# Mixer of an encoder block: wider token projections, decay products by direction, LayerNorm factors behind the transposes

## The chip, the cores and the metric

The kernel runs on one core of a Trainium2 chip. The metric is the device time of one launch in microseconds (us). Engines are named as the profile names them: PE is TensorE (PEld its weight loads), DVE is VectorE, ACT is ScalarE, POOL is GpSimd, SP is the engine whose queue issues most DMAs.

## The reference, cut to what matters

256 tokens (S) of 1024 channels (D), all float32. The block has two parts: a mixer with three branches, and 32 experts of which each token takes four.

```python
h = layer_norm(x, ln_in_g, ln_in_b)
mem_n = layer_norm(mem, ln_mem_g, ln_mem_b)
proj = h @ w_in + b_in          # q, k, v, r, lr_f, lr_b, fn, mq, gates
la_f = log_sigmoid(lr_f @ w_decay_f + b_decay_f) / 16    # lr_f: [256, 16]
la_b = log_sigmoid(lr_b @ w_decay_b + b_decay_b) / 16
# A) gated linear attention over q, k, v, la_f forward and over the flipped ones with la_b
# B) 2-D DFT of fn      C) cross-attention of mq into mem_n @ w_mem_kv
merged = g0 * y_gla + g1 * y_fnet + g2 * y_mem
h = layer_norm(alpha * h + merged @ w_out + b_out, ln1_g, ln1_b)
h = layer_norm(alpha * h + moe(h), ln2_g, ln2_b)
```

where `layer_norm(x) = (x - mean) * rsqrt(var + eps) * g + b`, by rows of 1024.

## The kernel before

The function `block` calls `mixer` and then `moe`. The experts' weights (2 MB a load) go into ten ring buffers; six of them are freed during the mixer and loaded early (`early_load`, line 777).

**Projections.** Every projection is done in split precision: ScalarE copies a weight chunk of 128x1024 into a rounded format (`whi`, line 117), VectorE subtracts to get the rest (`wlo`, line 118), and each product is three matmuls (`mm3`, lines 144 to 146): high by high, high by low, low by high. The activations h are kept split and transposed as `hT`, the memory as `mT`. There are four buffers of `whi` and of `wlo`, and three of raw weights.

`project_T` gives a result with channels on the partitions: the weight chunk is stationary, 256 tokens move. `project_tok` (line 325) gives a result with tokens on the partitions: 128 tokens of the activations are stationary, the weights move. It is called five times: twice for v, once for the memory's values, twice for the output projection. A call covers 512 columns as two halves of 256; each half is loaded as 8 chunks of K by 256 columns (1 MB), split in two pieces of four chunks, and multiplied for the first 128 tokens, then for the second. With `last` (the second output call) the second 128 tokens wait until the first have been handed on.

**Background.** Work that is not a projection is written as generators that are queued in `bg`. After each piece of a projection `bg.tick(1.05)` pays 1.05 us of debt, and a generator runs until it has yielded as much. The queue begins with `mem_norm_gen` (line 374), `decay_gen` (398), `mem_turn_gen` (384) and `gla_gen` (438). Outside of the blocks marked `manual_schedule` the framework places instructions of one engine in an order of its own by what it expects to be ready, so the trace need not follow the text; each engine works its own list strictly in order, except that TensorE loads weights ahead.

**Memory LayerNorm.** `mem_norm_gen` takes the statistics (line 87), and `ln_apply` with `cut=0` lets ScalarE normalise a tile of 128x1024 (line 100) and GpSimd multiply by g (101) and add b (102), both broadcast over the partitions by two DMAs (line 371). `mem_turn_gen` then transposes four blocks of 128x128 at a time into PSUM, and splits from there into `mT` (lines 117, 118, tiles mTh and mTl).

**Decays.** The low-rank part of the projection gives `lrT`, 32 rows (16 a direction) and a row of ones. `wd` (33 rows) holds for each direction its 16 rows of decay weights, zeros for the other direction, and its bias. Line 405 multiplies, 33 rows deep, for one direction and two heads at a time; the following passes (ACT lines 408, 411, 412; DVE lines 409, 413) make the logarithm, and a scan over 1024 columns per direction (line 418) the running sum. One such float32 matmul shows as two records in the trace.

**PSUM.** `pj` (projections) and `ms` (everything else) have four banks each.

Of the kernel before, what the change touches and what calls it, by code (L numbers as in the profile page):

```python
# [197 lines left out]
def mixer(ctx: ExitStack, K, A):  # L198
# [41 lines left out]
    brow = one.tile([64, 128], F32, name="brow")  # L240
    bT = one.tile([128, 64], F32, name="bT")
    blr = one.tile([32, 1], F32, name="blr")
    lrT = one.tile([33, S], F32, name="lrT")
    nc.gpsimd.memset(brow, 0.0)
    nc.gpsimd.memset(lrT[32:33], 1.0)
# [12 lines left out]
    for ap, src in ((blr, b_in[3072:3104].rearrange("(p c) -> p c", c=1)),  # L258
# [7 lines left out]
    with tc.manual_schedule(engines={mybir.EngineType.DVE, mybir.EngineType.PE, mybir.EngineType.Activation}):  # L266
# [26 lines left out]
        wlr_parts = split_w(K, wlr[:, :, :32])  # L293
# [31 lines left out]
    def project_tok(W, c0, X, evac, last=False, eng=None):  # L325
# [4 lines left out]
        def run(tau, half, parts):  # L330
            sl = slice(tau * 128, tau * 128 + 128)
            for k in range(8):
                hi, lo = parts[k // 4]
                mm3(K, ps[tau][:, half], X.at(k, sl), (hi[:, k % 4], lo[:, k % 4]), k == 0, k == 7)
# [12 lines left out]
        evac(0, ps[0].rearrange("p c n -> p (c n)"))  # L347
        if last:
            for half in range(2):
                run(1, half, allp[half])  # L350
        evac(1, ps[1].rearrange("p c n -> p (c n)"))
# [4 lines left out]
    for k in range(8):  # L356
        mm3(K, ps[:32, 0], (hi[:, k], lo[:, k]), hT.at(k), k == 0, k == 7)
    nc.vector.tensor_scalar(lrT[0:32], ps[0:32, 0], blr, None, ALU.add)
    psb = K.ps.tile([128, 64], F32, name="psb", tag="ms")
    nc.tensor.transpose(psb, brow, K.ident[:64, :64])  # L360
# [37 lines left out]
    def decay_gen():  # L398
        for d in range(2):
            la = at_part(d, part=part3)  # L400
            for hp in range(2):
                ps = K.ps.tile([128, 2, S], F32, name="lps", tag="ms")
                for j in range(2):
                    hh = hp * 2 + j
                    nc.tensor.matmul(ps[:, j], wd[:, d, hh * 128:(hh + 1) * 128], lrT, start=True, stop=True)
                e = gla[:, 2 + d, hp * 512:hp * 512 + 512].rearrange("p (j s) -> p j s", j=2)
                m = la[:, hp * 2:hp * 2 + 2]
# [923 lines left out]
```

## Time and profile before

| | |
|---|---|
| median of 3 runs | 1245.85 us (1245.77 to 1246.05) |
| profiled execution | 1244.73 us, span 1243.0 us |
| PE busy | 1174.9 us (95%), granted clock 0.979 of full on the mean |
| DVE, ACT, POOL busy | 386.8 us (31%), 254.6 us (20%), 59.4 us (5%) |
| read from HBM | 457.22 MB |
| first expert matmul | 329.0 us after the span's start |

A timeline's row has its start and length in us, the engine, the line of the kernel, the operation, what it writes and reads, shapes (partitions x elements) and count; in brackets stands how long the engine was idle before it, and what ended that. Rows of one kind that follow each other are merged, so that a length runs from the first one's start to the last one's end. The table of stretches gives each engine's busy time within a stretch, the TensorE clock that was granted (1.00 is 2.4 GHz, 0.50 is 1.2 GHz) and the mean share of the DMA engines that was in use.

### The profile page before, as it was taken

To read this page: it belongs to the slowest core of one execution; us is meant where nothing else is said; L and a number is where in the kernel's file an instruction comes from. 1 tells how busy PE (TensorE), PEld (TensorE's weight loads), DVE (VectorE), ACT (ScalarE), POOL (GpSimd) and SP (SyncE) were. 2 spreads that over 40 slices of the span, in tenths; PEclk is the share of its full clock that TensorE was granted. 3 is DMA by queue.
4 is the path that set the end of the run, shared out by engine and by line. 5 is a ranking of instruction groups with operands and counts; after the bars stand their busy time and mean duration, and the time that the engine had idled before them with its cause. 6 is when DMAs were issued, how large, how long until landed. Compare 5 with 4: busy or idle time off the path is not lost.

```text
span 1243.0 us, 15353 instructions
## 1 busy us (share of the span) xinstructions
PE 1174.9 (95%) x6653; PEld 651.8 (52%) x6653; DVE 386.8 (31%) x589; ACT 254.6 (20%) x436; POOL 59.4 (5%) x76
## 2 busy tenths in 40 slices
PE   7899999999999999999898989899989999898995
PEld 6799999999643443434243333334343424242432
DVE  7896455386411121211112020203111111111124
ACT  4655555553110110101011010101010101010110
POOL 3460000000100000000000000000000000000000
PEclk9899999999999999999999999989999999998998
DMA  8665566688899999999999999999999999999993
GB/s 300 203 208 171 204 204 216 225 322 292 335 376 422 424 431 429 431 431 430 430 430 432 431 430 430 431 431 429 431 430 430 431 430 430 431 430 430 428 421 128
DMA packets 80283, 459.31 MB, mean 370 GB/s; under 512 B 4662, under 2 KB 49264, under 8 KB 55508
## 3 DMA queue, kind: packets, MB, share of 16 engines
q1 hardware_dynamic: 79800, 457.66, 89.9%
q8 instruction: 54, 0.88, 0.3%
q10 hardware_dynamic: 284, 0.55, 0.1%
q14 instruction: 17, 0.14, 0.0%
q0 software_dynamic: 128, 0.07, 0.0%
HBM read 457.22 MB, written 1.05 MB: 369 GB/s over the span
## 4 chain that ended last, share of the span: by engine, by line
PE 63%; DMA 30%; DVE 4%; ACT 1%; issue 1%; SPq 0%; POOL 0%; DVEq 0%; ACTq 0%; POOLq 0%
DMA wexp<-in_w_down_dram 30%; PE gps L985 17%; PE yps L985 13%; PE pj L146 6%; PE pj L145 6%; PE pj L144 6%; PE mps L828 5%; PE gps L979 2%; PE yps L1055 1%; PE mps L1055 1%; DVE wlo L118 1%; PE gps L1024 1%; PE mps L1102 0%; DVE bst L87 0%; PE gps L932 0%
## 5 line engine op out<-in xcount | busy, mean ns | idle before, releaser
L985 PE MATMUL gps<-wexp,xT 128*64 128x512 f32 x1984 | 440.0, 593 | 6.9 <-DMA wexp<-in_w_gu_dram 6.6
L985 PEld LDWEIGHTS gps<-wexp,xT 128*64 128x64 f32 x1984 | 142.9, 137 | 299.6 <-issue 283.6
L985 PE MATMUL yps<-wexp,work 128*64 128x512 f32 x960 | 237.1, 625 | 31.7 <-DMA wexp<-in_w_down_dram 31.6
L985 PEld LDWEIGHTS yps<-wexp,work 128*64 128x64 f32 x960 | 71.9, 143 | 194.3 <-issue 143.5
L790 DVE TENSOR_SCALAR sg<-gps 128x512 f32<-128x512 f32 x31 | 21.3, 688 | 422.4 <-PE gps L985 389.1
L118 DVE TENSOR_TENSOR wlo<-wraw,whi 128x1024 fp32r<-128x1024 f32 (+2 forms) x97 | 118.3, 1228 | 63.7 <-ACT whi L117 63.6
L117 ACT ACTIVATE whi<-wraw 128x1024 fp32r<-128x1024 f32 (+2 forms) x97 | 94.9, 985 | 97.5 <-PE pj L145 82.3
L791 ACT ACTIVATE sg<-sg 128x512 f32<-128x512 f32 x32 | 20.2, 632 | 458.2 <-DVE sg L790 458.2
L144 PE MATMUL pj<-hT,whi 128*128 128x256 f32 (+1 forms) x392 | 112.0, 286 | 0.0
L146 PE MATMUL pj<-hT,wlo 128*128 128x256 f32 (+1 forms) x392 | 110.4, 282 | 0.5 <-DVE wlo L118 0.5
L145 PE MATMUL pj<-hT,whi 128*128 128x256 f32 (+1 forms) x392 | 110.3, 281 | 0.5 <-DVE hT L118 0.5
L1031 DVE SCALAR_TENSOR_TENSOR y<-yps,sw,y 128x512 fp32r<-128x512 f32 x30 | 22.5, 751 | 232.4 <-ACT y L1030 231.4
L146 PEld LDWEIGHTS pj<-hT,wlo 128*128 128x128 f32 (+1 forms) x392 | 73.2, 187 | 1.0 <-DVE wlo L118 0.9
L145 PEld LDWEIGHTS pj<-hT,whi 128*128 128x128 f32 (+1 forms) x392 | 73.2, 187 | 1.0 <-DVE hT L118 0.8
L144 PEld LDWEIGHTS pj<-hT,whi 128*128 128x128 f32 (+1 forms) x392 | 73.2, 187 | 0.9 <-ACT whi L117 0.3
L1030 ACT ACTIVATE y<-yps,sw 128x512 fp32r<-128x512 f32 x30 | 20.6, 688 | 240.0 <-PE yps L985 230.9
L828 PEld LDWEIGHTS mps<-P,h 128*128 128x128 f32 x512 | 61.6, 196 | 12.7 <-issue 12.2
L828 PE MATMUL mps<-P,h 128*128 128x128 f32 x512 | 64.8, 285 | 0.4 <-DVE P L821 0.4
L976 POOL COPY sel<-kp 128x128 f32<-128x128 f32 x32 | 9.5, 296 | 809.5 <-PE yps L979 448.0
L1059 DVE TENSOR_TENSOR sum<-sum,yps 128x512 f32<-128x512 f32 (+1 forms) x30 | 18.8, 667 | 71.4 <-PE yps L1055 71.4
L919 ACT ACTIVATE xT<-mps 128x512 f32<-128x512 f32 x32 | 19.2, 599 | 58.8 <-PE mps L828 58.8
L145 PE MATMUL pj<-wlo,hT 128*128 128x256 f32 x64 | 19.1, 299 | 4.2 <-DVE wlo L118 4.2
(278 smaller groups left out, 1156.0 us busy)
## 6 DMA issues: line engine op xcount, KB each, us to landing
wexp<-in_w_gu_dram SPq DMA_DIRECT2D x127, 2048.0 KB, 36.4
wexp<-in_w_down_dram SPq DMA_DIRECT2D x60, 2048.0 KB, 35.1
wraw<-in_w_in_dram SPq DMA_DIRECT2D x28, 1024.0 KB, 5.1
wexp<-in_w_down_dram SPq DMA_DIRECT2D x8, 768.0 KB, 28.0
wraw<-in_w_mem_kv_dram SPq DMA_DIRECT2D x4, 1024.0 KB, 4.9
wraw<-in_w_br_gla_dram SPq DMA_DIRECT2D x4, 1024.0 KB, 6.7
wraw<-in_w_out_dram SPq DMA_DIRECT2D x4, 1024.0 KB, 5.1
wraw<-in_w_br_fnet_dram SPq DMA_DIRECT2D x2, 1024.0 KB
```

Source lines behind the costliest of these rows:

```text
L117: K.nc.scalar.activation(hi, src, AF.Copy)
L118: K.nc.vector.tensor_tensor(lo, src, hi.bitcast(F32), ALU.subtract)
L144: nc.tensor.matmul(out, wh, xh, start=first, stop=False)
L145: nc.tensor.matmul(out, wh, xl, start=False, stop=False)
L146: nc.tensor.matmul(out, wl, xh, start=False, stop=last)
L790: nc.vector.tensor_scalar(g, gate, 7.0, None, ALU.min)
L828: nc.tensor.matmul(t[:, c], h1[tau][:, f0 + c % 2:f0 + 256:2], P[:, tau].rearrange("p e s -> p (e s)"), start=first and c == 0, stop=last, ...
L979: nc.tensor.matmul(ac, t[r].rearrange("k e s -> k (e s)"), bias[r, c0:c0 + ac.shape[-1]], start=first, stop=not first, skip_group_check=True)
L985: nc.tensor.matmul(acc[e * 64:e * 64 + 64], xT[:, k, e * 64:e * 64 + 64], w[e], start=first, stop=last, skip_group_check=True)
L1030: nc.scalar.activation(y[:, 0, sl], acc, AF.Copy, scale=w)
L1031: nc.vector.scalar_tensor_tensor(y[:, 1, sl], acc, w, y[:, 0, sl].bitcast(F32), ALU.mult, ALU.subtract)
L1055: nc.tensor.matmul(c, G[:, tau * 128:tau * 128 + 128], y[:, i, sl], start=i == 0, stop=i == 1)
```

## The change

`project_tok` loads its 512 columns as two loads of four K chunks by 512 columns (1 MB each, as before). A split takes two K chunks of 512 columns (1024 elements, as before). For each split, both groups of 128 tokens are multiplied, with 512 moving columns. One tick follows each split.

The decay weights of the two directions lie on partitions 0 to 16 and 32 to 48 (16 rows of weights and a bias row each); the low-rank projection has 48 columns in place of 32, so that its result lies on these partitions too, and `lrT` is filled with ones first. For a pair of heads, the products of both directions are issued by turns, 17 rows deep. The two scans come behind all of this.

The memory's g and b come as 8 rows each into the small tile `brow`, which is transposed to `bT` (channels on partitions). ScalarE still normalises; GpSimd's two passes and the broadcast loads go. After a transpose, ScalarE applies g and b to each block of 128x128, from PSUM into SBUF, and the split reads SBUF.

```diff
-    lrT = one.tile([33, S], F32, name="lrT")
-    nc.gpsimd.memset(brow, 0.0)
-    nc.gpsimd.memset(lrT[32:33], 1.0)
+    lrT = one.tile([64, S], F32, name="lrT")
+    nc.gpsimd.memset(lrT, 1.0)
...
-    for ap, src in ((blr, b_in[3072:3104].rearrange("(p c) -> p c", c=1)),
+    for ap, src in ((blr[0:16], b_in[3072:3088].rearrange("(p c) -> p c", c=1)),
+                    (blr[32:48], b_in[3088:3104].rearrange("(p c) -> p c", c=1)),
+                    (brow[58:66], A["ln_mem_g"].rearrange("(c p) -> c p", p=128)),
+                    (brow[66:74], A["ln_mem_b"].rearrange("(c p) -> c p", p=128)),
...
-        wlr_parts = split_w(K, wlr[:, :, :32])
+        wlr_parts = [K.wspl.tile([128, 1024], F32R, name=n, tag=n)[:, :384].rearrange("p (k n) -> p k n", k=8)
+                     for n in ("whi", "wlo")]
+        for to, fr in ((slice(0, 32), slice(0, 32)), (slice(32, 48), slice(16, 32))):
+            split(K, wlr[:, :, fr], *[t[:, :, to] for t in wlr_parts])
...
-    wd = gla[:33, 1].rearrange("p (d n) -> p d n", d=2)
-    nc.gpsimd.memset(wd, 0.0)
+    wd = gla[:64, 1, 0:512]
     for d, name in enumerate(("decay_f", "decay_b")):
-        nc.gpsimd.dma_start(wd[d * 16:d * 16 + 16, d], A["w_" + name][0])
-        nc.gpsimd.dma_start(wd[32:33, d], A["b_" + name])
+        nc.gpsimd.dma_start(wd[d * 32:d * 32 + 16], A["w_" + name][0])
+        nc.gpsimd.dma_start(wd[d * 32 + 16:d * 32 + 17], A["b_" + name])
...
-        ws = [load_w(K, W, c0 + half * 256, 256, 8) for half in range(2)]
-        ps = [K.ps.tile([128, 2, 256], F32, name="pj", tag="pj") for _ in range(2)]
+        ws = []
+        for h in range(2):
+            w = K.wraw.tile([128, 2048], F32, name="wraw", tag="wraw").rearrange("p (k n) -> p k n", k=4)
+            nc.sync.dma_start(w, W[h * 512:h * 512 + 512, c0:c0 + 512].rearrange("(k p) n -> p k n", p=128))
+            ws.append(w)
+        ps = [K.ps.tile([128, 512], F32, name="pj", tag="pj") for _ in range(2)]
...
-        for half in range(2):
-            parts = [split_w(K, ws[half][:, i * 4:i * 4 + 4]) for i in range(2)]
-            allp.append(parts)
-            run(0, half, parts)
-            bg.tick(TICK)
-            if not last:
-                run(1, half, parts)
-                bg.tick(TICK)
+        for k in range(0, 8, 2):
+            parts = split_w(K, ws[k // 4][:, k % 4:k % 4 + 2])
+            allp.append(parts)
+            for tau in range(1 if last else 2):
+                for i in range(2):
+                    run(tau, k + i, parts)
+            bg.tick(K.TICK)
...
-    nc.vector.tensor_scalar(lrT[0:32], ps[0:32, 0], blr, None, ALU.add)
+    for r in (slice(0, 16), slice(32, 48)):
+        nc.vector.tensor_scalar(lrT[r], ps[r, 0], blr[r], None, ALU.add)
...
-    gm, bm = part2[:, 0], part2[:, 1]
-    for t, src in ((gm, A["ln_mem_g"]), (bm, A["ln_mem_b"])):
-        nc.sync.dma_start(t, src[None, :].broadcast_to([128, D]))
...
-            ln_apply(K, xm[tau], ms[tau], rs[tau], gm, bm, xm[tau], 0)
-            yield 0.1
+            t = K.small.tile([128, 8], F32, name="nmr", tag="sm")[:, 0:1]
+            nc.vector.scalar_tensor_tensor(t, ms[tau][:, 0:1], -1.0, rs[tau], ALU.mult, ALU.mult)
+            nc.scalar.activation(xm[tau], xm[tau], AF.Identity, bias=t, scale=rs[tau])
+            yield 0.2
...
-                transpose_split(K, xm[tau], tau, mT, j)
+                ps = K.ps.tile([128, 4, 128], F32, name="tps", tag="ms")
+                t = part2[:, tau, j * 512:j * 512 + 512].rearrange("p (c n) -> p c n", c=4)
+                for c in range(4):
+                    cc = j * 4 + c
+                    nc.tensor.transpose(ps[:, c], xm[tau][:, cc * 128:cc * 128 + 128], K.ident)
+                for c in range(4):
+                    cc = j * 4 + c
+                    nc.scalar.activation(t[:, c], ps[:, c], AF.Identity, bias=bT[:, 66 + cc:67 + cc],
+                                         scale=bT[:, 58 + cc:59 + cc])
+                sl = slice(tau * 128, tau * 128 + 128)
+                split(K, t, mT.hi[j][:, :, sl], mT.lo[j][:, :, sl])
...
-        for d in range(2):
-            la = at_part(d, part=part3)
-            for hp in range(2):
-                ps = K.ps.tile([128, 2, S], F32, name="lps", tag="ms")
-                for j in range(2):
-                    hh = hp * 2 + j
-                    nc.tensor.matmul(ps[:, j], wd[:, d, hh * 128:(hh + 1) * 128], lrT, start=True, stop=True)
+        las = [at_part(d, part=part3) for d in range(2)]
+        for hp in range(2):
+            pss = [K.ps.tile([128, 2, S], F32, name="lps", tag="ms") for _ in range(2)]
+            for j in range(2):
+                hh = hp * 2 + j
+                for d in range(2):
+                    rows = slice(d * 32, d * 32 + 17)
+                    nc.tensor.matmul(pss[d][:, j], wd[rows, hh * 128:(hh + 1) * 128], lrT[rows], start=True, stop=True)
```

## Rows read from the trace of the kernel before

**Rows 1.** Waits of the DMA queue on SP, 330:372 us: us, times, longest

```profile
SPq L777 <- PE yps L985: 21.6, 3, 12.1
```

**Rows 2.** Stretches: length, busy PE PEld DVE ACT POOL, clock, DMA share, GB/s

```profile
30.00:60.00 30.00, 25.83 (x170) 23.39 (x169) 26.72 (x36) 17.18 (x26) 13.30 (x6) 0.89 0.63 213
60.00:90.00 30.00, 29.50 (x249) 29.05 (x248) 29.23 (x24) 18.65 (x23) 18.74 (x10) 1.00 0.58 194
180.00:210.00 30.00, 30.00 (x258) 30.00 (x258) 19.22 (x27) 16.96 (x29) 0.00 (x0) 1.00 0.62 210
```

**Rows 3.** Waits of TensorE, 15 to 320 us: us in total, times, longest

```profile
PE pj L145 <- DVE wlo L118: 4.2, 1, 4.2
PE pj L146 <- DVE wlo L118: 0.7, 3, 0.3
```

**Rows 4.** GpSimd's timeline: start us, us, operation, idle before it

```profile
37.66 2.77 POOL L101 TENSOR_TENSOR m<-m,parts 128x1024 f32<-128x1024 f32 x1 [2.42 <-ACT m L100]
45.79 4.21 POOL L102 TENSOR_TENSOR m<-m,parts 128x1024 f32<-128x1024 f32 x1
70.78 2.85 POOL L464 TENSOR_TENSOR gla<-gla,parts 128x1024 f32<-128x1024 f32 x1
```

**Rows 5.** VectorE's timeline

```profile
15.42 0.42 DVE L118 TENSOR_TENSOR wlo<-wraw,whi 128x256 fp32r<-128x256 f32 x1
...
38.09 2.35 DVE L99 SCALAR_TENSOR_TENSOR nmr<-bmv,rsy 128x1 f32<-128x1 f32 x1
...
42.28 1.17 DVE L413 TENSOR_TENSOR parts<-parts,gla 128x512 f32<-128x512 f32 x1 [1.24 <-ACT gla L412]
43.49 4.37 DVE L418 TENSOR_TENSOR_SCAN parts<-gla,parts 128x1024 f32<-128x1024 f32 x1
47.78 4.44 DVE L118 TENSOR_TENSOR wlo<-wraw,whi 128x1024 fp32r<-128x1024 f32 x2
...
60.54 2.29 DVE L418 TENSOR_TENSOR_SCAN parts<-gla,parts 128x1024 f32<-128x1024 f32 x1
62.75 2.34 DVE L118 TENSOR_TENSOR wlo<-wraw,whi 128x1024 fp32r<-128x1024 f32 x2
...
71.29 0.68 DVE L118 TENSOR_TENSOR mTl<-tps,mTh 128x512 fp32r<-128x512 f32 x1
71.89 2.82 DVE L118 TENSOR_TENSOR wlo<-wraw,whi 128x1024 fp32r<-128x1024 f32 x1
```

**Rows 6.** TensorE's timeline, the stretch behind its long wait

```profile
51.14 0.58 PE L145 MATMUL pj<-wlo,hT 128*128 128x256 f32 x1 [4.17 <-DVE wlo L118]
...
57.97 0.28 PE L145 MATMUL pj<-wlo,hT 128*128 128x256 f32 x1
```

**Rows 7.** Busy time by stretches of 1 us, columns as in rows 2

```profile
55.00:56.00 1.00, 1.00 (x6) 1.00 (x6) 1.00 (x2) 0.00 (x0) 0.00 (x0) 0.50 1.09 387
```

**Rows 8.** TensorE's timeline, projection matmuls and a decay group at full clock

```profile
25.78 0.28 PE L146 MATMUL pj<-hT,wlo 128*128 128x256 f32 x1
...
31.46 0.28 PE L146 MATMUL pj<-hT,wlo 128*128 128x256 f32 x1
31.67 1.13 PE L405 MATMUL lps<-lrT,gla 33*128 33x256 f32 x4
```

**Rows 9.** ScalarE's timeline

```profile
68.82 0.58 ACT L117 ACTIVATE mTh<-tps 128x512 fp32r<-128x512 f32 x1
...
86.14 0.82 ACT L499 ACTIVATE parts<-pj,bT 128x256 f32<-128x256 f32 x2
```

**Rows 10.** Experts: line 1055's durations (ns min/median/max), then TensorE's timeline

```profile
L1055 PE MATMUL mps<-y,G x12: 388/389/393, 517.8 to 629.1; 128*128 128x512 f32 x12
...
627.36 1.17 PE L1055 MATMUL yps<-y,G 128*128 128x512 f32 x4
628.37 1.07 PE L1055 MATMUL mps<-y,G 128*128 128x512 f32 x4
629.38 1.14 PE L979 MATMUL gps<-ebias,sel 32*128 32x512 f32 x8
```

More of the change, by code (lines that the diff above doesn't have):

```diff
@@ L239, in mixer @@
     chan, amask = cm[:, 0:128], [cm[:, 128:256], cm[:, 256:384]]
-    brow = one.tile([64, 128], F32, name="brow")
-    bT = one.tile([128, 64], F32, name="bT")
-    blr = one.tile([32, 1], F32, name="blr")
-    lrT = one.tile([33, S], F32, name="lrT")
-    nc.gpsimd.memset(brow, 0.0)
-    nc.gpsimd.memset(lrT[32:33], 1.0)
+    brow = one.tile([74, 128], F32, name="brow")
+    bT = one.tile([128, 74], F32, name="bT")
+    blr = one.tile([48, 1], F32, name="blr")
+    lrT = one.tile([64, S], F32, name="lrT")
+    nc.gpsimd.memset(lrT, 1.0)
     hTt = K.early.tile([128, 4, 4, S], F32R, name="hT", tag="ring3")
@@ L323, in project_T, with project_tok, run @@
                     bg.tick(TICK * kn / 8)
-    def project_tok(W, c0, X, evac, last=False, eng=None):
-        ws = [load_w(K, W, c0 + half * 256, 256, 8) for half in range(2)]
-        ps = [K.ps.tile([128, 2, 256], F32, name="pj", tag="pj") for _ in range(2)]
[L330 to L334, printed above, removed]
+    def project_tok(W, c0, X, evac, last=False):
+        ws = []
[4 more added lines that the diff above has]
+        ps = [K.ps.tile([128, 512], F32, name="pj", tag="pj") for _ in range(2)]
+        def run(tau, k, parts):
+            hi, lo = parts
+            mm3(K, ps[tau], X.at(k, slice(tau * 128, tau * 128 + 128)), (hi[:, k % 2], lo[:, k % 2]), k == 0, k == 7)
         allp = []
-        for half in range(2):
-            parts = [split_w(K, ws[half][:, i * 4:i * 4 + 4]) for i in range(2)]
+        for k in range(0, 8, 2):
+            parts = split_w(K, ws[k // 4][:, k % 4:k % 4 + 2])
             allp.append(parts)
-            run(0, half, parts)
-            bg.tick(TICK)
-            if not last:
-                run(1, half, parts)
-                bg.tick(TICK)
+            for tau in range(1 if last else 2):
+                for i in range(2):
+                    run(tau, k + i, parts)
+            bg.tick(K.TICK)
         if last:
@@ L346, in project_tok @@
             K.order.__enter__()
-        evac(0, ps[0].rearrange("p c n -> p (c n)"))
+        evac(0, ps[0])
         if last:
-            for half in range(2):
-                run(1, half, allp[half])
-        evac(1, ps[1].rearrange("p c n -> p (c n)"))
+            for k in range(8):
+                run(1, k, allp[k // 2])
+        evac(1, ps[1])
     ps = K.ps.tile([128, 2, S], F32, name="pj", tag="pj")
@@ L356, in mixer @@
     for k in range(8):
-        mm3(K, ps[:32, 0], (hi[:, k], lo[:, k]), hT.at(k), k == 0, k == 7)
-    nc.vector.tensor_scalar(lrT[0:32], ps[0:32, 0], blr, None, ALU.add)
-    psb = K.ps.tile([128, 64], F32, name="psb", tag="ms")
-    nc.tensor.transpose(psb, brow, K.ident[:64, :64])
+        mm3(K, ps[:48, 0], (hi[:, k], lo[:, k]), hT.at(k), k == 0, k == 7)
+    for r in (slice(0, 16), slice(32, 48)):
+        nc.vector.tensor_scalar(lrT[r], ps[r, 0], blr[r], None, ALU.add)
+    psb = K.ps.tile([128, 74], F32, name="psb", tag="ms")
+    nc.tensor.transpose(psb, brow, K.ident[:74, :74])
     nc.vector.tensor_copy(bT, psb)
@@ L398, in decay_gen @@
     def decay_gen():
-        for d in range(2):
-            la = at_part(d, part=part3)
-            for hp in range(2):
-                ps = K.ps.tile([128, 2, S], F32, name="lps", tag="ms")
-                for j in range(2):
-                    hh = hp * 2 + j
-                    nc.tensor.matmul(ps[:, j], wd[:, d, hh * 128:(hh + 1) * 128], lrT, start=True, stop=True)
+        las = [at_part(d, part=part3) for d in range(2)]
[6 more added lines that the diff above has]
+                    nc.tensor.matmul(pss[d][:, j], wd[rows, hh * 128:(hh + 1) * 128], lrT[rows], start=True, stop=True)
+            for d in range(2):
                 e = gla[:, 2 + d, hp * 512:hp * 512 + 512].rearrange("p (j s) -> p j s", j=2)
-                m = la[:, hp * 2:hp * 2 + 2]
-                nc.scalar.activation(e, ps, AF.Abs)
-                nc.vector.tensor_scalar(m, ps, 0.0, None, ALU.min)
+                m = las[d][:, hp * 2:hp * 2 + 2]
+                nc.scalar.activation(e, pss[d], AF.Abs)
+                nc.vector.tensor_scalar(m, pss[d], 0.0, None, ALU.min)
                 yield 0.7
@@ L414, in decay_gen @@
                 yield 0.7
+        for d in range(2):
+            la = las[d]
             r = slice(None) if d == 0 else slice(None, None, -1)
```

## The prediction, made before the changed kernel ran

> **What bounds the kernel now.** I read the busy time by stretches of 30 us first, then who waits for whom on the DMA queue and on TensorE, then the timelines of VectorE, GpSimd and TensorE around the one long wait. The kernel is two kernels in a row: the mixer, up to about 329 us, and the experts behind it. In the experts, loads are issued when TensorE gives a buffer back: over 330 to 372 us the queue's longest wait is for the expert matmuls, 21.6 us [rows 1]. In the mixer the DMA engines have room, 0.58 to 0.63 of their time [rows 2]. So what the mixer's end gains, I let through to the end one for one.
>
> Inside the mixer TensorE is full: 29.50 of 30 us, then 30.00 of 30 [rows 2]. Only 30 to 60 us is short, with 25.83 us at a mean granted clock of 0.89. There lies TensorE's one long wait, 4.2 us for VectorE's low half of a split weight (wlo); its other waits for a wlo make 0.7 us [rows 3]. VectorE is nearly full as well, 26.72 us of 30 to 60 and 29.23 us of 60 to 90 [rows 2]. Two engines run neck and neck up to about 95 us; behind that only TensorE counts. The working has therefore two sums, and the smaller decides.
>
> **Memory LayerNorm.** It takes four GpSimd passes of 128x1024 off (lines 101 and 102), which run one behind the other from 37.66 to 50.00 us [rows 4], and two broadcast loads off SP's queue. In exactly these 12 us VectorE is slow [rows 5]: a 128x1 operation (nmr) takes 2.35 us and ends at 40.44, where GpSimd's first pass ends (40.43); the scan takes 4.37 us, against 2.29 us for the same scan at 60.54; two wlo take 4.44 us, against 2.34 us for the pair at 62.75. That is 2.1 us (I leave the small one 0.25 us), 2.1 us and 2.1 us: 6.3 us lost. A further 1.24 us at 42.28 is VectorE waiting for ScalarE, which I read as the nmr's delay passed on: the second normalisation (line 100) needs it and stands in ScalarE's order ahead of that pass. Without the passes the wlo comes some 7.5 us earlier than 51.1 us, at 43.6; TensorE asks for it at 51.14 - 4.17 = 46.97 [rows 6]. The wait goes, with 3 us to spare.
>
> With it goes the slow clock behind it. After the 4.17 us of idleness the granted clock was 0.50, that is 1.2 of 2.4 GHz [rows 7]. From 51.14 to 57.97 us TensorE did 23 projection matmuls, one group of decay matmuls and one matmul more [rows 6]. At full clock these take 23 x 0.118 + 1.13 + 0.23 = 4.1 us (0.118 is the pace of 49 matmuls from 25.78 to 31.46, 5.68 us over 48 steps; 1.13 the decay group at 31.67 [rows 8]) in place of 6.83: 2.7 us. Wait and clock make **6.9 us** of TensorE's time.
>
> What it adds: the scaling moves behind the turns (the transposes of memory), as 16 ScalarE passes of 128x128 out of PSUM. Two of 128x256 take 0.82 us, one of 128x512 takes 0.58 us [rows 9], so I estimate 0.33 us for 128 columns and 5.3 us in all. ScalarE has them: it is busy 18.65 us of 60 to 90 [rows 2]. I cost them at nothing; without that cover all 5.3 us would be late. The turn's data is first needed by the key projection of the memory, behind the whole value projection.
>
> One thing speaks against it. At 71.29 us the low half of a turn took 0.68 us although GpSimd was in a pass (70.78 to 73.63); the next operation, a wlo with both inputs in SBUF, took 2.82 us [rows 4, 5]. The turn's low half read PSUM; in the new code it reads SBUF twice, so it may be held as the wlo was. The passes of lines 463 and 464 stay. Bounds over four turns: 0 if none coincides, 4 x 0.68 = 2.7 us if each loses what it now runs under a pass. I take the middle, 1.4 us, on VectorE. The Trainium skill, page "SBUF — State Buffer", section "SBUF: two separate sides", says the same as a rule: a VectorE operation with two SBUF inputs and a GpSimd operation that reads SBUF exclude each other for a whole instruction. By it the high bound holds wherever they meet, which would make the forecast 1.3 us later.
>
> **Decays by direction.** Sixteen records in four groups of four become two groups of eight, the two directions in different row groups. One group of four takes 1.13 us [rows 8]. That row groups overlap is to be seen at the experts' biases: four matmuls of 512 columns in four row groups, eight records, take 1.14 us [rows 10], about what four records of half the columns take in one group. So I take 1.1 us for each new group: 4 x 1.1 - 2 x 1.1 = **2.2 us** saved. If they did not overlap, a group of eight would take some 1.9 us and 0.6 us would be left; more than 2.2 the rows do not allow. The scans of both directions come later and close together, 2 x 2.29 us, and a new group holds two of the four small PSUM tiles at once; both cost nothing as long as split weights are ahead (rival 2 prices it). The extra columns of the low-rank weights need a second split at the start, on the chain: 0.42 us for 256 columns [rows 5], so 0.3 us lost for 128. The three further small loads go out of ScalarE's queue before it has a pass to run, since its first one needs the statistics of x; SP issues two loads fewer and GpSimd two fills fewer; I count that as nothing, since no wait for them is on record.
>
> **512 moving columns.** Five calls with 96 matmuls of 256 columns each become 48 of 512: 240 pairs. A pair costs 2 x 0.1183 = 0.2366 us [rows 8]. The nearest matmul of 512 columns in this number format is the combine (line 1055): four span 1.07 us with the 0.39 us of the last, so (1.07 - 0.39)/3 = 0.227 us per step [rows 10]. Saved: 9.6 ns a pair, 2.3 us in all, 0.9 in the two value calls and 1.4 in the other three. Bounds: whole groups stand 628.37 - 627.36 = 1.01 us apart, 0.2525 for each of four [rows 10], which would lose 3.8 us; at the other end the rounding of the rows leaves 0.224, 3.0 us saved. I take the step inside a group, because here one matmul follows the other for long. Splits, loads and background ticks stay as many. "TensorE: Matmul & The Clock Gate" in the Trainium skill, section "Back-to-back issue gap", gives N/2.4 + 2.5 ns a matmul; an estimate by it saves 2.5 ns a pair, 0.6 us in all, and would make the forecast 1.7 us later. The trace differs: 118.3 ns in the row where the skill's formula has 109.2.
>
> **The sum.** TensorE up to 95 us: 6.9 + 2.2 + 0.9 - 0.3 = 9.7 us. VectorE up to 95 us: 6.3 + 1.24 - 0.3 - 1.4 = 5.8, and of its other idle time (30 - 26.72 + 30 - 29.23 = 4.05, less 1.24: 2.8 us, partly spent waiting for a TensorE on the slow clock) half, 1.4: 7.2 us. The smaller, 7.2, holds; TensorE gives 2.5 us back in short waits for wlo. The other three calls add 1.4: **8.6 us**. The profiled execution took 1244.73 us (span 1243.0 us); 1236.1 follows. The median of the three runs stands 1.1 us above it, so I forecast 1237.3.
>
> **Rivals.**
> 1. *VectorE keeps up* and TensorE's sum holds: 9.7 + 1.4 and the 0.7 us of other waits for wlo [rows 3] = 11.8 us, 1234.0. For it: VectorE's load drops by more than the turns add. Against: 29.23 us busy of 30. Chance 0.17.
> 2. *The wait comes back elsewhere.* Two scans and the decays' other passes close together leave VectorE 4.6 us and more without a wlo; TensorE stands idle as long as now and the clock falls again. 6.9 us are lost again, 1.7 remain: 1244.2. Against: one prepared split feeds 24 matmuls, 2.8 us, and several can be ahead. Chance 0.12.
> 3. *Slower.* ScalarE works in order. A turn now holds it for 0.58 + 4 x 0.33 = 1.9 us, and longer when its transposes are late; the high half of the next weight stands behind it, VectorE behind that. If the first and a later turn (66 to 80 us today) each starve TensorE past the 2.8 us of one prepared split, long enough for the clock to fall, each costs 6.9 us: 13.8 - 8.6 = 5.2 us slower, 1251.0. Against: ScalarE idles 11 us of those 30. Chance 0.08.
> 4. *The change does less than it says:* 512 columns at 0.2525 us and no overlap of row groups, 2.3 + 3.8 + 1.6 = 7.7 us less on TensorE, of which its lead over VectorE hides 2.5: 3.4 us gained, 1242.4. Chance 0.08.
> 5. *Hidden anyway:* the experts' loads turn out bound by DMA from the mixer's tail on, and no gain arrives: 1245.8. Against: the waits of [rows 1]. Chance 0.05.
>
> **Numbers.** The forecast has 0.50. About 0.2% (2.5 us) is what a measurement of this kernel can tell from no change. Faster: forecast, 1 and 4, 0.75; same: 2 and 5, 0.17; slower: 3, 0.08. The range 1233.3 to 1244.5 reaches from rival 1 with the 0.7 us of the 512 bound past rival 4 and just past rival 2; it leaves out 3 and 5, 0.13, and the far ends of what it holds.
>
> **What would show it.** Right: no GpSimd pass between 35 and 50 us; nmr, scan and wlo there at 0.2, 2.3 and 1.2 us; no wait of TensorE above 1 us and clock 1.00 through 30 to 60; decay groups of eight in 1.1 us; 512-column steps of 0.227 us; the first expert matmul near 320.5 us in place of 329.0. Wrong: a wait for wlo above 3 us anywhere, a stretch at 0.50, turns that hold ScalarE while wlo is late, or an experts' part that is longer than before.

## The result, and the profile after

The changed kernel takes 1235.97 us (median of 4 runs, 1235.02 to 1236.97), the kernel before beside it 1245.95 us (4 runs, 1245.77 to 1247.47): a ratio of 0.9919, 95% interval [0.9905, 0.9933]. That is 10.0 us faster, where 8.6 were forecast. The profiled executions took 1244.73 and 1235.43 us, with spans of 1243.0 and 1233.5 us.

The stretches of 30 us of the kernel after, columns as in [rows 2] (busy PE, PEld, DVE, ACT, POOL, granted clock, DMA share, GB/s):

```profile
30.00:60.00 30.00, 30.00 (x199) 26.51 (x199) 27.77 (x43) 21.95 (x32) 3.00 (x5) 1.00 0.77 261
60.00:90.00 30.00, 29.56 (x205) 26.96 (x204) 30.00 (x22) 22.80 (x39) 18.93 (x8) 1.00 0.55 179
```

TensorE is now full from 30 to 60 us, at 1.00 (2.4 GHz); it had been busy 25.83 us there at 0.89. VectorE is busy for all of 60 to 90 us, a little more than before. TensorE's waits for split weights from 15 to 320 us, 4.9 us in [rows 3], are these:

```profile
PE pj L146 <- DVE wlo L118: 0.4, 2, 0.2
```

VectorE's timeline of the kernel after:

```profile
37.83 0.15 DVE L385 SCALAR_TENSOR_TENSOR nmr<-bmv,rsy 128x1 f32<-128x1 f32 x1
...
48.22 4.47 DVE L437 TENSOR_TENSOR_SCAN parts<-gla,parts 128x1024 f32<-128x1024 f32 x2
52.60 1.20 DVE L118 TENSOR_TENSOR wlo<-wraw,whi 128x1024 fp32r<-128x1024 f32 x1
...
60.13 2.84 DVE L118 TENSOR_TENSOR wlo<-wraw,whi 128x1024 fp32r<-128x1024 f32 x1
62.89 0.68 DVE L495 TENSOR_TENSOR parts<-pj,bv 128x512 f32<-128x512 f32 x1
63.49 2.83 DVE L118 TENSOR_TENSOR wlo<-wraw,whi 128x1024 fp32r<-128x1024 f32 x1
...
70.33 1.28 DVE L118 TENSOR_TENSOR mTl<-parts,mTh 128x512 fp32r<-128x512 f32 x2
...
74.47 15.67 DVE L118 TENSOR_TENSOR wlo<-wraw,whi 128x1024 fp32r<-128x1024 f32 x7
```

The nmr takes 0.15 us (2.35 in [rows 5]), both scans together 4.47 us (2.24 each; beside a pass of GpSimd, one took 4.37 in [rows 5]), a wlo 1.20 us. From 60 us on a wlo takes 2.84, 2.83 and then, over seven, 2.24 us on the mean. GpSimd's timeline of the same kernel says beside what:

```profile
57.99 0.99 POOL L581 MEMSET parts<- 128x512 f32 x2 [21.07 <-DVE gla L478]
59.10 2.79 POOL L482 TENSOR_TENSOR gla<-gla,parts 128x1024 f32<-128x1024 f32 x1
61.84 3.40 POOL L483 TENSOR_TENSOR gla<-gla,parts 128x1024 f32<-128x1024 f32 x1
...
72.96 6.02 POOL L666 TENSOR_TENSOR h<-h,parts 128x1024 f32<-128x1024 f32 x2 [2.64 <-DMA parts<-in_b_out_dram]
78.93 3.39 POOL L482 TENSOR_TENSOR gla<-gla,parts 128x1024 f32<-128x1024 f32 x1
82.28 3.38 POOL L483 TENSOR_TENSOR gla<-gla,parts 128x1024 f32<-128x1024 f32 x1
```

From 37 to 58 us GpSimd does nothing. Its six other passes (four multiplications for the inner products, two additions of the output bias to the residual) are still there, and VectorE is held beside each. Other rows: a decay group has eight records in 1.13 us at 33.37 and at 43.17 us; the first q leaves PSUM at 27.78 us (26.10 before); the first expert matmul starts at 319.83 us, 9.18 us earlier than before, and the span is 9.5 us shorter. So what the mixer gained did reach the end.

### The profile page after: what moved, and what is told of

Same layout as the page of the kernel before. It is cut to its first block, busy times and chain, and to the rows that moved or that the text cites. A ratio compares the mean times of both kernels' runs of the same rounds, so it can differ in the third digit from the quotient of the medians.

```text
span 1233.5 us, 14884 instructions
## 1 busy us (share of the span) xinstructions
PE 1168.8 (95%) x6413; PEld 639.0 (52%) x6413; DVE 381.5 (31%) x591; ACT 259.0 (21%) x453; POOL 47.4 (4%) x70
## 4 chain that ended last, share of the span: by engine, by line
PE 66%; DMA 29%; DVE 2%; ACT 1%; issue 0%; SPq 0%; POOL 0%; DVEq 0%; ACTq 0%
DMA wexp<-in_w_down_dram 25%; PE gps L1004 19%; PE yps L1004 13%; PE pj L146 7%; PE pj L144 7%; PE pj L145 6%; PE mps L847 5%; DMA wexp<-in_w_gu_dram 3%; PE gps L998 2%; PE yps L1074 1%; PE mps L1074 1%; PE gps L1043 1%; DVE wlo L118 1%; PE yps L998 0%; PE mps L1121 0%
## 5 line engine op out<-in xcount | busy, mean ns | idle before, releaser
L1004 PE MATMUL yps<-wexp,work 128*64 128x512 f32 x960 | 234.5, 622 | 32.3 <-DMA wexp<-in_w_down_dram 32.3
L812 DVE TENSOR_TENSOR sg<-sg 128x512 f32<-128x512 f32 x32 | 22.1, 690 | 3.2 <-ACT sg L810 1.6
```

The lines of the kernel that those rows point to most:

```text
L812: nc.vector.tensor_tensor(g, g, s, ALU.mult)
L1004: nc.tensor.matmul(acc[e * 64:e * 64 + 64], xT[:, k, e * 64:e * 64 + 64], w[e], start=first, stop=last, skip_group_check=True)
```

## The experiments

The question after the result was why. The forecast was a sum of parts; does each give its own term? Code is cut to what matters; a minus stands for the kernel that the text starts from (the changed kernel where it names none), a plus for the run. In the table the first three columns say which parts a kernel has. "Waits" are TensorE's for wlo from 30 to 95 us. "q to expert" is the time from the first q out of PSUM to the first expert matmul, in the profiled execution, so that the start of the kernel is left out. The last two rows are the changed kernel with small edits told below; by them and the kernel after, this time scatters by some 0.5 us between near copies.

| kernel | LayerNorm | 512 | decays | median us | ratio to before, 95% | waits us | q to expert us |
|---|---|---|---|---|---|---|---|
| before | | | | 1245.95 | | 4.9 | 302.9 |
| b1_ln_only | x | | | 1245.93 | 1.000 [0.9991, 1.001] | 5.4 | 302.8 |
| b2_tok512_only | | x | | 1243.34 | 0.9978 [0.9968, 0.9987] | 4.1 | 303.7 |
| b3_decay_only | | | x | 1245.17 | 0.9990 [0.9981, 1.000] | 4.3 | 300.4 |
| u3_decay_back | x | x | | 1244.84 | 0.9988 [0.9979, 0.9998] | 5.7 | 301.1 |
| u1_tok256 | x | | x | 1239.94 | 0.9945 [0.9932, 0.9958] | 2.9 | 296.7 |
| u2_gpsimd_ln | | x | x | 1241.25 | 0.9962 [0.9948, 0.9976] | 4.1 | 297.4 |
| after | x | x | x | 1235.97 | 0.9919 [0.9905, 0.9933] | 0.4 | 292.1 |
| b4_vec10 | no GpSimd pass | | | 1238.48 | 0.9937 [0.9923, 0.9951] | 0 | 294.2 |
| u6_back_quiet | x | x | (no GpSimd pass) | 1235.75 | 0.9908 [0.9893, 0.9923] | 0 | 293.1 |
| u7_back_memset | x | x | (fills only) | | | 0 | 293.1 |
| u8_vec6 | x | x | x (no GpSimd pass) | 1236.20 | 0.9919 [0.9907, 0.9932] | 0 | 290.8 |
| u4_loads_sp | x | x | x | 1235.99 | 0.9916 [0.9903, 0.9929] | 0.4 | 292.2 |
| u5_dir_seq | x | x | x | 1235.34 | 0.9917 [0.9904, 0.9929] | 0.5 | 291.7 |

**One part undone: projections at 256 columns.**

```diff
-        for k in range(0, 8, 2):
-            parts = split_w(K, ws[k // 4][:, k % 4:k % 4 + 2])
+        for half in range(2):
+            parts = [split_w(K, ws[half][:, i * 4:i * 4 + 4]) for i in range(2)]
```

> The changed kernel with the token projections back at 256 moving columns (two halves, as before); the other parts stay. The prediction's size of this part (9.6 ns a pair, 240 pairs): 2.3 us slower than the changed kernel, 1238.3 us. By the step of 0.2333 us that the changed kernel's profile shows for 512 columns against 0.1178 for 256 (2.3 to 3.3 ns a pair): 0.6 to 0.8 us slower, 1236.7 us. A third theory, that spreading the splits evenly over the matmuls is what keeps VectorE from being late, wants waits of TensorE for a low half to come back in the two value calls, 1 us or more in sum, and a clock below 1.00.

It cost 4.0 us, not 0.8. The clock stayed at 1.00, but waits came back in the value projection. TensorE's timeline of u1_tok256:

```profile
67.47 0.38 PE L145 MATMUL pj<-wlo,hT 128*128 128x256 f32 x1 [1.06 <-DVE wlo L118]
70.80 0.39 PE L145 MATMUL pj<-wlo,hT 128*128 128x256 f32 x1 [1.62 <-DVE wlo L118]
```

Of the two signs that the theory of the even spread of the splits asked for, the waits came and the lower clock did not. What is shown is that the pace of the matmuls is the small part of what the 512 columns are worth here, and that without them waits return; that it is the spread of the splits, and not the other order of loads and products, was not tried by itself.

**One part undone: the memory's LayerNorm with GpSimd's passes.**

```diff
-            nc.scalar.activation(xm[tau], xm[tau], AF.Identity, bias=t, scale=rs[tau])
+            ln_apply(K, xm[tau], ms[tau], rs[tau], gm, bm, xm[tau], 0)
```

> The changed kernel with memory's LayerNorm as before: g and b by GpSimd over 128x1024, the turn's split out of PSUM, the two broadcast loads back; the decays by direction and the 512 columns stay, and so do the small loads of g and b, which nothing uses then. If GpSimd's passes held VectorE and that made TensorE's wait: VectorE's operations of 0.2, 2.3 and 1.2 us again take 2 us and more longer where they meet a pass, TensorE waits 3 us or more once, a stretch at clock 0.50 follows, and the time is 5 to 7 us above the changed kernel, 1241 to 1243 us. If the wait went because of the new order of the decays or of the splits: no wait above 1 us and 1236 to 1237 us.

It cost 5.3 us. One wait of 4.1 us is back, and the granted clock was 0.96 from 30 to 60 us and 0.92 from 60 to 90. That is as the theory of the held VectorE had it, but the wait, from 55.7 to 59.8 us, comes later than in the kernel before. VectorE's timeline of u2_gpsimd_ln:

```profile
42.00 8.79 DVE L118 TENSOR_TENSOR wlo<-wraw,whi 128x1024 fp32r<-128x1024 f32 x3 [1.25 <-ACT whi L117]
...
54.13 4.46 DVE L429 TENSOR_TENSOR_SCAN parts<-gla,parts 128x1024 f32<-128x1024 f32 x2
```

Three wlo take 8.79 us beside GpSimd's passes, which end at 53.05 us. TensorE then waits while VectorE does both scans at their own pace: the passes made VectorE late, and the scans standing together (rival 2) set where that was felt.

**One part undone: the decays in four groups, one direction after the other.**

```diff
-                for d in range(2):
-                    rows = slice(d * 32, d * 32 + 17)
-                    nc.tensor.matmul(pss[d][:, j], wd[rows, hh * 128:(hh + 1) * 128], lrT[rows], start=True, stop=True)
+                nc.tensor.matmul(ps[:, j], wd[:, d, hh * 128:(hh + 1) * 128], lrT, start=True, stop=True)
```

> The changed kernel with the decays as before: 33 rows, one direction after the other, 32 low-rank columns, one split at the start, one small load fewer. If row groups overlap: decay groups of four records take 1.1 us again, four of them, 2.2 us more on TensorE; the start gets 0.3 us back from the split and perhaps 0.5 us from the small load, so 1.4 to 1.9 us above the changed kernel, 1237.4 to 1237.9 us. If the overlap were worth nothing: 0.3 to 0.8 us below it, 1235.2 to 1235.7 us. If the scans of both directions close together were what hurts VectorE, waits for a low half would shrink, but they make 0.4 us in the changed kernel, so no more than that.

This cost 8.9 us, over four times what was expected. VectorE's timeline of u3_decay_back, then GpSimd's:

```profile
64.67 2.89 DVE L464 TENSOR_TENSOR x<-x,parts 128x512 f32<-128x512 f32 x1
...
72.35 2.56 DVE L118 TENSOR_TENSOR mTl<-parts,mTh 128x512 fp32r<-128x512 f32 x1
74.83 3.40 DVE L118 TENSOR_TENSOR wlo<-wraw,whi 128x1024 fp32r<-128x1024 f32 x1
78.15 0.68 DVE L487 TENSOR_TENSOR parts<-pj,bv 128x512 f32<-128x512 f32 x1
78.75 2.81 DVE L118 TENSOR_TENSOR wlo<-wraw,whi 128x1024 fp32r<-128x1024 f32 x1
81.49 2.88 DVE L465 TENSOR_TENSOR x<-x,parts 128x512 f32<-128x512 f32 x1
```

```profile
64.23 2.77 POOL L474 TENSOR_TENSOR gla<-gla,parts 128x1024 f32<-128x1024 f32 x1
...
71.94 2.42 POOL L475 TENSOR_TENSOR gla<-gla,parts 128x1024 f32<-128x1024 f32 x1 [1.60 <-ACT gla L472]
74.31 6.17 POOL L658 TENSOR_TENSOR h<-h,parts 128x1024 f32<-128x1024 f32 x2
80.44 3.38 POOL L474 TENSOR_TENSOR gla<-gla,parts 128x1024 f32<-128x1024 f32 x1
```

Operations that take 0.7 or 1.2 us take 2.6 to 3.4 us beside GpSimd, one low half of a turn (mTl) among them, and TensorE waits 5.7 us at 78 to 88 us. The stretch from 60 to 90 has TensorE at 24.33 of 30 us. Undone one by one, the parts cost 4.0, 5.3 and 8.9 us, 18.1 in all before rounding (17 by the ratios), where all three together are worth 10.0. They are not terms of a sum.

**The three added small loads.** They go to SP's queue, behind the first weights:

```diff
-                    (blr[32:48], b_in[3088:3104].rearrange("(p c) -> p c", c=1)),
+    for ap, src in ((blr[32:48], b_in[3088:3104].rearrange("(p c) -> p c", c=1)),
...
+        nc.sync.dma_start(ap, src)
```

> The changed kernel with its three added small loads (half of the low-rank bias, memory's g and b) issued from SP behind the first weights, no longer from ScalarE's queue at the very start. Theory: they delay the second half of x, which lands at 6.60 us in the changed kernel against 4.9 us or so before, and with it everything, 1.4 to 1.7 us. Then the second statistics start at 6.2 us, the first q leaves PSUM near 26.4 us in place of 27.78, and the time is 1.2 to 1.6 us lower, 1234.5 us. Rival: the late start is the second split of the low-rank weights (0.3 us) and chance: 27.3 to 27.8 us and no more than 0.3 us lower, 1235.8 us.

1235.99 us, [0.9903, 0.9929], first q at 27.64 us: no gain, so these loads do not make the start late.

**One part done alone, three times.** The kernel before with the LayerNorm part, the 512 columns or the decays' part of the diff. The last two also keep the small loads of the memory's g and b, which nothing uses there.

> The kernel before with the LayerNorm part alone (its factors behind the turns). Three theories. (1) Parts that add up: it is worth its own terms, the wait of 4.2 us, the clock's 2.7 and a little more: 1239 +- 1.5, no wait of TensorE over 1 us from 30 to 95 us. (2) VectorE's work from 58 to 95 us is the common bound: the wait at 47 us goes, the clock there stays at 1.00, but TensorE meets VectorE again in the 58 to 95 us stretch and gives most of it back: 1242 to 1246, waits on low halves of 3 us or more there. By the sums of the three undone parts (18.1 us against 10.0 for all), the three parts alone are together worth about 2 us if they interact only in pairs. (3) Only the undone decays' order was bad by accident: then this part alone still gives 1239 to 1241.

> The kernel before with the projections by token at 512 columns alone. Adding up: 0.6 to 0.8 us from the steps, so 1245 to 1245.5. Common bound: the wait of 4.2 us near 47 us and the clock's loss stay, the splits spread evenly take at most a part of what VectorE is late: 1243 to 1246. If the even spread is worth its 3 us whatever the rest: 1242.

> The kernel before with the decays' products by direction alone. Adding up by undoing: 8.9 us, 1237. By the rows of the products (two groups of eight in 1.13 us in place of four groups of four): 1.4 to 1.9 us, less 1.0 us at the start: 1244 to 1245.5. Common bound: 1243 to 1247, with the wait near 47 us still there at 3 us or more.

The LayerNorm part, which the forecast paid with 6.9 us of TensorE's time, is alone worth nothing. Stretches and waits of b1_ln_only:

```profile
30.00:60.00 30.00, 30.00 (x229) 27.91 (x227) 25.71 (x40) 19.68 (x28) 1.11 (x2) 1.00 0.73 232
60.00:90.00 30.00, 24.60 (x193) 24.19 (x192) 30.00 (x22) 21.35 (x36) 18.44 (x10) 0.94 0.44 151
```

```profile
PE pj L146 <- DVE wlo L118: 5.4, 2, 3.9
```

The first half of the prediction's step happens exactly as written: 30.00 of 30 us at 1.00. Then the wait and the slow clock come again 28 us later, where VectorE is full and GpSimd's other passes run. VectorE's timeline of b1_ln_only shows who is held there:

```profile
69.86 5.70 DVE L118 TENSOR_TENSOR mTl<-parts,mTh 128x512 fp32r<-128x512 f32 x2
...
76.08 2.77 DVE L118 TENSOR_TENSOR wlo<-wraw,whi 128x1024 fp32r<-128x1024 f32 x1
78.77 2.85 DVE L118 TENSOR_TENSOR mTl<-parts,mTh 128x512 fp32r<-128x512 f32 x1
```

The turns' low halves, which this part makes read SBUF twice, are held beside passes: three of the four take 2.85 to 2.89 us, where all four took 0.68 to 0.69 us in the kernel before. That is 6.6 us more of VectorE's time, about the 6.3 us that the removed passes had cost it, and two of the three stand just ahead of the wlo at 76.08 for which TensorE waits until 78.90 us. So the part does not only uncover the next place; it also gives GpSimd's other passes more to hold. How much of the new wait is due to which was not separated.

The 512 columns alone give 2.6 to 2.7 us, 1243.34 us, at the near end of what the common bound allows and short of the even spread's 1242. Where they come from its trace does not show: the profiled execution, at 1246.95 us, is the slowest of its 11. The decays alone give 0.8 to 0.9 us, at the edge of the noise; 1245.17 us lies in the range expected by their rows less the start and in that of the common bound, so it does not tell them apart. In its profiled execution 2.5 us less from q to expert stand against a first q that came 2.6 us later, and a wait of 3.2 us ends at 58.78 us.

**Without GpSimd's passes.** In u6_back_quiet the six passes from 58 to 95 us are left out of u3_decay_back (its q and k of the inner products are not multiplied, and the output's bias is not added):

```diff
-            nc.gpsimd.tensor_tensor(kin[d], kin[d], kT, ALU.mult)
-            nc.gpsimd.tensor_tensor(qin[d], qin[d], qT, ALU.mult)
...
-            nc.gpsimd.tensor_tensor(hs[tau], hs[tau], bo, ALU.add)
```

> The changed kernel with the decays as before, as in u3_decay_back, and GpSimd's six passes from 58 to 95 us left out: the four multiplications of the inner products' q and k by the raw q and k, and the two additions of the output bias to the residual. If these passes hold VectorE (its rows of 2.6 to 3.4 us there against 0.7 to 1.2 alone) and so cause the 5.7 us of waits that u3_decay_back had at 78 to 88 us, the waits fall below 1.5 us, TensorE is busy over 28 of the 30 us from 60 to 90, and the time falls by 4 to 7 us to 1238 to 1241. If it is the order of VectorE's list that makes TensorE wait, whoever shares the memory with it, waits and time stay: 1243 to 1245.5.

1235.75 us, 9.1 us less than u3_decay_back, more than expected, and not one wait. With these passes gone the old form of the decays causes no wait. Its stretch from 60 to 90 us:

```profile
60.00:90.00 30.00, 30.00 (x213) 27.81 (x212) 21.59 (x25) 23.82 (x40) 1.99 (x4) 1.00 0.69 233
```

VectorE has 21.59 us of work there, where u3_decay_back showed 29.88. Most of those 8 us of "busy" time was being held, not working.

**Fills in their place.**

```diff
-            nc.gpsimd.tensor_tensor(kin[d], kin[d], kT, ALU.mult)
-            nc.gpsimd.tensor_tensor(qin[d], qin[d], qT, ALU.mult)
+            for t in (kin[d], qin[d]):
+                for _ in range(3):
+                    nc.gpsimd.memset(t, 1.0)
...
-            nc.gpsimd.tensor_tensor(hs[tau], hs[tau], bo, ALU.add)
+            for _ in range(3):
+                nc.gpsimd.memset(hs[tau], 1.0)
```

> u6_back_quiet with 18 fills by GpSimd in place of the six passes left out (three of 128x1024 for each, some 0.96 us each, so about as long), at the same places and into the same tiles; the values of q, k and the residual are not the reference's. GpSimd then only writes. If what holds VectorE is that GpSimd reads two operands from the memory that both use, the fills hold nothing: 1235 to 1237, VectorE's passes at 0.7 and 1.2 us. If any use of that memory by GpSimd holds it: rows of 2.3 to 3.4 us again, waits of 4 to 6 us, 1241 to 1246.

The time, 5625 us, answers nothing: the fills overwrite the residual too, tokens become alike, and the experts' overflow loop ran (thousands of matmuls that no other kernel here has), presumably since too many tokens chose the same experts. Up to the first expert matmul, at 320.37 us, the mixer can be read. GpSimd's timeline, then VectorE's:

```profile
21.35 5.46 POOL L660 MEMSET h<- 128x1024 f32 x6 [0.58 <-PE pj L145]
...
72.35 2.98 POOL L476 MEMSET gla<- 128x1024 f32 x3 [3.71 <-ACT gla L472]
77.18 5.68 POOL L476 MEMSET gla<- 128x1024 f32 x6 [1.85 <-ACT gla L471]
```

```profile
72.84 0.69 DVE L118 TENSOR_TENSOR mTl<-parts,mTh 128x512 fp32r<-128x512 f32 x1 [0.17 <-ACT mTh L117]
73.80 1.23 DVE L118 TENSOR_TENSOR wlo<-wraw,whi 128x1024 fp32r<-128x1024 f32 x1 [0.26 <-ACT whi L117]
...
77.27 2.35 DVE L118 TENSOR_TENSOR wlo<-wraw,whi 128x1024 fp32r<-128x1024 f32 x2
80.00 1.23 DVE L118 TENSOR_TENSOR wlo<-wraw,whi 128x1024 fp32r<-128x1024 f32 x1 [0.37 <-ACT whi L117]
```

The six fills in place of the residual's additions ran at 21 us and not where those passes stand, so twelve of the 18, for q and k from 64.7 to 82.9 us, are the test. Beside them VectorE runs at its own pace, and from first q to first expert the kernel takes 293.1 us, as with nothing in their place. GpSimd writing this memory does not hold VectorE; its passes that also read two operands from it do. The Trainium skill, page "SBUF — State Buffer", section "SBUF: two separate sides", has it as a rule: a VectorE operation with two SBUF inputs and a GpSimd operation that reads SBUF exclude each other for whole instructions. The trace agrees on each side of it: 2.56 us for a turn's low half beside a pass (u3_decay_back), 0.69 us for one beside a fill, and 0.68 us for the row at 62.89 of the kernel after, which has one input in PSUM and ran inside a pass.

**The passes on VectorE.** The kernel before, with no part of the change, but with all ten passes done by VectorE (the LayerNorm's four become two passes of VectorE for each half in place of ScalarE's one and GpSimd's two):

```diff
-            ln_apply(K, xm[tau], ms[tau], rs[tau], gm, bm, xm[tau], 0)
+            ln_apply(K, xm[tau], ms[tau], rs[tau], gm, bm, xm[tau], D)
...
-            nc.gpsimd.tensor_tensor(kin[d], kin[d], kT, ALU.mult)
+            nc.vector.tensor_tensor(kin[d], kin[d], kT, ALU.mult)
...
```

> The kernel before, with no part of the change, but with GpSimd's ten passes over 128x1024 from 35 to 95 us done by VectorE (the memory's LayerNorm by two passes of VectorE for each half in place of one of ScalarE and two of GpSimd; four multiplications and two additions as they are). If GpSimd's passes hold VectorE and that is the whole cause of TensorE's waits, VectorE has more work of its own and still ends sooner: no wait of TensorE over 1.5 us from 30 to 95 us, clock 1.00 there, 1236.5 to 1240. If VectorE's load itself is the cause, its 12 to 13 us of added passes make the waits longer: 1246 to 1253.

1238.48 us (6 runs, 1235.82 to 1239.85): 7.5 us of the change's 10.0 without any of its three parts. Stretches of b4_vec10:

```profile
30.00:60.00 30.00, 30.00 (x227) 27.50 (x227) 28.94 (x41) 18.71 (x27) 1.11 (x2) 1.00 0.77 261
60.00:90.00 30.00, 30.00 (x258) 30.00 (x258) 28.54 (x32) 19.56 (x24) 1.98 (x4) 1.00 0.70 233
```

VectorE does ten passes more than in the kernel before. From 30 to 60 us, with the LayerNorm's, it is busy 28.94 us (26.72 in [rows 2]); from 60 to 90, with the six others, 28.54 us, less than the 29.23 of [rows 2]. TensorE never waits for a wlo. ScalarE loses its two normalisations by this edit as well, which was not tried apart. The same on the changed kernel, for its six passes:

> The changed kernel with GpSimd's six passes from 58 to 95 us done by VectorE. VectorE's 30.00 us of 30 from 60 to 90 should fall to 26 to 28, but TensorE waited only 0.4 us there, so the time should stay within 0.5 us of the changed kernel's, 1235.4 to 1236.4. Over 1 us of gain would say that TensorE still loses time on VectorE that the waits do not show; over 1 us of loss, that VectorE's own load is near the bound.

1236.20 us: the same as the kernel after, as expected, with VectorE at 27.65 us from 60 to 90. From first q to first expert it is 1.3 us quicker, but the rest of the execution was longer by 2.4 us: TensorE's waits for the experts' weights came to 40.7 us in that execution and 39.3 in the kernel after's. Over the profiled executions of all kernels but u7_back_memset the time from the first expert matmul to the end lies between 913.5 and 916.1 us, with the two kernels' 914.0 (before) and 913.7 (after) in it; a gain of 1 us in the mixer does not show through that scatter.

**Row groups one after the other.**

```diff
-            for j in range(2):
-                hh = hp * 2 + j
-                for d in range(2):
+            for d in range(2):
+                for j in range(2):
+                    hh = hp * 2 + j
```

> The changed kernel with the decays' eight products of a group in the order of the directions, four of the rows 0 to 16 and then four of the rows 32 to 48, no longer by turns. If products that follow each other on different rows overlap, a group of eight takes about twice the 1.13 us of a group of four, 1.9 to 2.3 us in place of 1.13, twice: 1.5 to 2.3 us more, 1237.5 to 1238.3. If the order within a group is indifferent: 1236 and 1.13 us. If the cut of VectorE's order is what the decays' part is worth, the time stays at 1236 as well, and the groups take 1.9 us or more.

1235.34 us, [0.9904, 0.9929], the same as after, and the groups of eight took 1.14 us. The expectation of 1.9 us fell. TensorE's timeline of u5_dir_seq:

```profile
32.40 1.14 PE L421 MATMUL lps<-lrT,gla 17*128 17x256 f32 x8
33.47 0.38 PE L144 MATMUL pj<-hT,whi 128*128 128x256 f32 x1
```

The records of the group start in pairs throughout, although the program hands over both products of one direction before the first of the other. (The second of a pair starts 13 to 14 ns behind the first, where it was 6 to 7 in the kernel after, so something of the new order did arrive.) What the decays' part needs is the different rows, not the turns.

## Why the prediction was right, and where its steps were off

**Wait and clock, 6.9 us: right where it looked, wrong as a term.** The rows that it rested on came as forecast: no GpSimd pass from 37 to 58 us; nmr, scan and wlo at 0.15, 2.24 and 1.20 us; no wait over 1 us; 1.00 in the stretch. But b1_ln_only shows that this part alone earns nothing: the wait of 47 to 51 us is gone, and one of 75 to 79 us is there. Taking the cause away at one place left the same cause (GpSimd's other passes) at the next, and put the turns' low halves beside it. The prediction asked where TensorE would be late next, and answered with a smooth loss of 2.5 us; without the other two parts it is a new wait of 3.9 us and a new stretch at a lower clock.

**Decays, 2.2 us: the rows as forecast, and confirmed by difference.** Two groups of 1.13 us stand in place of four. Between kernels without waits, u6_back_quiet and u8_vec6, the time from q to expert falls by 293.13 - 290.76 = 2.4 us (the removed groups take 2 x 1.13 = 2.3). Their whole times do not differ (1235.75 and 1236.20 us): in u8_vec6 the first q came 1.7 us later and the experts took 0.7 us longer. What the prediction did not have is the other effect. With the old order of the decays VectorE was busy 25.68 us from 30 to 60 us in u3_decay_back, against 27.77 in the kernel after, and had more left to do beside GpSimd's passes. That the earlier work is what helps was not tried by itself; that GpSimd's passes are what makes the old order dear is shown by u6_back_quiet.

**512 columns, 2.3 us: mis-sized.** TensorE's timeline of the kernel after, first and last of 21 matmuls:

```profile
300.60 0.39 PE L144 MATMUL pj<-whi,mg0h 128*128 128x512 f32 x1
...
305.26 0.40 PE L146 MATMUL pj<-whi,mg1l 128*128 128x512 f32 x1
```

4.66 us over 20 steps is 0.2330 us, not the 0.227 taken from the experts' combine [rows 10]. That was a group too short for a difference of some ns: by the trace of the kernel before, the last seven of its eight matmuls start from 627.68 to 629.06 us, 0.230 us apart on the mean. Against 0.2366 the 0.2330 saves 3.6 ns a pair, 0.9 us in all. The Trainium skill, page "TensorE: Matmul & The Clock Gate", section "Back-to-back issue gap", gives N/2.4 + 2.5 ns for a matmul by itself at full clock; the trace differs in both steps (by the formula 215.8 and 109.2 ns, in these rows 233.0 and 118.3). Yet the estimate by it, 2.5 ns a pair, was nearer than the prediction's 9.6. The new order of splits and products, which the prediction counted as "splits stay as many" and no more, made up for it: undone, it brings waits of 2.9 us in place of 0.4.

**The turns' low halves, 1.4 us on VectorE: none was charged, and the upper bound was wrong.** The four took 0.68 us each in the kernel after: three ran between the passes, and the last, from 72.67 us, was under way when a pass began at 72.96. The mechanism is real, as the 2.56 us of u3_decay_back and three times 2.85 us and more in b1_ln_only show. The bound of 4 x 0.68 = 2.7 us took a half to lose no more than its own length; each of those three lost 2.2 us, 6.6 us together. The prediction gave no reason why none would be held, so that nothing was paid here is luck.

**"The smaller, 7.2, holds": failed.** VectorE kept up, as in rival 1; TensorE gave back 0.4 us in waits, not 2.5. From q to expert the gain is 302.9 - 292.1 = 10.8 us (the parts below round to 10.9), against TensorE's forecast sum of 9.7 + 0.3 (no start) + 1.4 = 11.4 us. By the runs without waits it consists of 302.9 - 294.2 = 8.7 us that GpSimd's passes cost before, less 292.1 - 290.8 = 1.3 us that they still cost, 2.4 us of the decays, and 294.2 - 293.1 = 1.1 us for the 512 columns and the LayerNorm's new place. With a scatter of some 0.5 us the two small terms are rough.

**The start, 0.3 us: too small.** The first q came 1.7 us later. In seven kernels with the decays' new layout it comes at 26.88 to 28.68 us (27.7 on the mean), in seven without at 25.76 to 27.98 (26.8). So about 0.9 us seems to belong to the layout and the rest to that execution; in the kernel after VectorE also waited 0.46 us for the g of the first LayerNorm. The scatter is as large as the difference, and it stays open.

That the total came near is partly luck, since the errors nearly cancel: 8.6, and 2.5 that VectorE did not take, less 1.4 of the 512 columns and 1.4 of the start, make 8.3, where the first expert matmul came 9.2 us earlier; the 0.9 us left over is not assigned. That the gain arises before 95 us and passes through the experts one for one was right, within the 2.6 us by which the experts' time scatters. Rival 3 did not come: a turn's four scaling passes take 1.48 us of ScalarE (0.37 each, where 0.33 was estimated), and ScalarE is busy 22.80 us of 60 to 90. Rival 2, the wait that returns elsewhere, did not happen in the kernel after, but a wait does return elsewhere when the LayerNorm part stands alone and when either other part is missing: in full in u3_decay_back, in u1_tok256 with 1.6 us at the longest and no lower clock. The mechanism that rival 2 named, both scans without a wlo between them, shows in u2_gpsimd_ln.

## What to carry to other kernels

Where VectorE and GpSimd both work on the same memory, look for operations of VectorE that take two to four times their own length, and try GpSimd's reading passes on VectorE first: here the kernel was 7.5 us faster with ten passes more on VectorE. Ask also which operations a change makes newly liable to be held, as the turns' low halves were here. A part of a change that removes a wait is worth what the next wait allows; do each part alone as well as undo it, since here the undone parts added up to 18 us and the parts alone to under 4. Measure a matmul's step in a long row of the same kind, not in a group of four.

## What the runs showed of the hardware that was not expected

Products on different rows of TensorE overlapped without being handed over by turns: both products of rows 0 to 16 and then both of rows 32 to 48 took 1.14 us, as long as one direction's two products (33 rows deep) take in the kernel before, 1.13 us [rows 8]. And GpSimd's fills of 128x1024, 0.95 to 0.96 us each, did not slow VectorE's operations beside them, where beside GpSimd's passes with two operands the same operations took two to four times as long (1.2 us became 2.8 to 3.4, 0.68 became 2.5 to 2.9).
